# Mixer A's short tiles with both heads in one double bank, and late group norms finished one by one

## The chip, the cores and the metric

The kernel runs on one core of one Trainium2 chip. The metric is the device time of one execution in microseconds; the kernel before is given by the median of three runs. A profile is one further execution, taken by the hardware profiler, with its own time. TensorE (PE in the profile) does the matrix products, with its weight loads listed apart (PEld); VectorE (DVE), ScalarE (ACT) and GpSimd (POOL) do the elementwise work; SyncE (SP) issues the transfers.

## What is computed

One layer of a streaming encoder over 1024 prompt frames and 32 sample frames, with 1024 columns: a SwiGLU block, two attention mixers side by side, and a second SwiGLU block, each between a norm before it and a norm after it. What bears on the change is the middle part:

```python
qa, ka, va, qb, kb, vb = jnp.split(h @ w_in, SPLITS, axis=-1)
oa, ob, rows = mixers(qa, ka, va, qb, kb, vb)
o = jnp.concatenate([rmsnorm(oa, group_gains[:WIDTH_A]),
                     rmsnorm(ob, group_gains[WIDTH_A:])], axis=-1) @ w_out

def band_attn_a(q, k, v, bias, valid):          # mixer A: 8 heads x 64
    s = jnp.einsum('bnqhd,bnkhd->bnhqk', q, k) * SCALE + bias
    s = jnp.where(valid[None, :, None], s, NEG_INF)
    p = jax.nn.softmax(s, axis=-1)
    return jnp.einsum('bnhqk,bnkhd->bnqhd', p, v)
```

In mixer A a frame reads its own chunk of 64 frames and the eight chunks ahead of it, with a learned bias by distance. Mixer B is a narrower window with 8 query heads on 2 key heads. `o` is the concatenation of two normed groups of 512 columns: group 0 is mixer A's output, group 1 mixer B's.

## The kernel before

Columns stand on the partitions and frames along the free axis. Frames are cut into three blocks `tb`: 384, 384 and 288 (256 prompt frames and the 32 sample frames). Products of activations and weights are made with each operand split into a high and a low part, three products for one (`mm3`, lines 342 to 344: high by high, weight's high by the activation's low, weight's low by the activation's high). The weights are split on the chip as they arrive: ScalarE writes the high part (line 320), VectorE the low part (line 321).

**The attention part.** It goes through 72 tiles in a list written out by hand: mixer B's four pairs of heads, then mixer A's pairs 0 and 1, one after the other, then A's pairs 2 and 3 interleaved (numbers 54 to 71). A pair is one `TileS` (the sample frames) and eight tiles of 128 prompt frames, i = 0 to 7. A `TileA` with i = 0, 1, 2, 3 has L = 128, 256, 384, 512 keys; these are called the short tiles here. From i = 4 on L is 640. A tile has four steps:
- `pre` (POOL, lines 1104 and 1105): the queries of both heads into `qz`, zeros in the other head's rows.
- `qk(h)`, once for each head: the scores on PE into `S`, a PSUM double bank (line 1115), the bias added (DVE, 1117), the negated maximum (DVE, 1121), the exponential with its sum (ACT, 1124), the reciprocal (DVE, 1125), and the scaling of P (ACT 1127 or DVE 1129 in turn).
- `tr(h)`: P transposed on PE in blocks of 128 (`pp`, line 1139) and copied out (`evac`: ACT line 1068, every fifth DVE line 1066).
- `av`: P times V on PE (`po`, line 1076), and the copy of the result into `O`, again by `evac`.

`qk` of a tile comes one tile ahead of its `tr` and `av`; while pairs 0 and 1 run, the projections of later pairs (`pq`) are put between the tiles. PSUM is cut into three pools: `p2`, two double banks that hold scores; `p1`, three single banks; `pc`, one single bank.

**The output part.** `group_norm(tb, g)` norms a group of 512 columns of a block. ScalarE squares (line 381) two pairs of column tiles, `sumsq` adds the two of a pair (the fold, line 385) and the earlier pair to it (line 387), on POOL or DVE by the table `SQE`; PE sums over the partitions (`pss`, line 374); twelve small operations on DVE make the reciprocal root (lines 405 to 408 and 351 to 355, here the chain of the root); PE spreads it over the partitions (`pr`, line 422); ScalarE copies it to `rstd` (line 1523); DVE makes `z` (line 1528), ScalarE its high part `o_hi` (line 1532), and the low part `o_lo` (line 1533) is made on POOL for the first half and on DVE for the second. `out_piece` makes one 128-column piece of the product with `w_out` for one block (24 products `wo`), for which it needs both groups of the block.

**What sets the order.** The side jobs (norms, residuals) are generators in a list: `begin` puts one at its end, or with `first=True` at its front; `step` advances the frontmost; `need(key)` steps until one is done. The norms of group 1 are begun at tile 55. Group 0 of block 0 is begun at tile 63, of block 1 at tile 69, of block 2 after the last tile. Five output pieces go between the last tiles, the other nineteen after them. The tile library then assigns buffers, adds the waits, and orders the instructions of each engine by a simulated timeline of its own; each engine runs its own row of instructions in that order.

## Time and profile before

| what | value |
|---|---|
| runs | 2183.55, 2179.83, 2183.74 us, median 2183.55 |
| the profiled execution's own time | 2187.33 us |
| its span | 2185.4 us |
| its mean granted TensorE clock | 0.986 |
| PE, DVE, ACT, POOL busy | 2122.6, 1392.4, 778.5, 169.2 us |

A row of the groups reads: line, engine, operation, output and input with partitions by elements, count, busy time and mean of one, then the idle time of the engine ahead of them with what ended it. A row of the timeline reads: start, duration, engine, line, operation, count, and in brackets the wait ahead of it. A row of the windows gives the busy time of PE, PEld, DVE, ACT and POOL in a stretch with the count of instructions, then the granted clock, the share of the DMA engines and GB/s. The places of this text in that execution: pair 0 of mixer A opens at about 1065 us, pairs 2 and 3 at 1215 us, their first long tile is scored at 1254.8 us, the last `po` of the attention part runs at 1328 us, and the second SwiGLU block follows the norms from about 1350 us on.

### The profile page before, as it was taken

The numbers are of one execution on the slowest core, as the hardware profiler recorded it, in microseconds if no ns is written. First come the engines' busy times: TensorE is split into PE (matmuls) and PEld (weight loads), VectorE is DVE, ScalarE is ACT, GpSimd is POOL, SyncE is SP. The second block draws the span as 40 slices with busy tenths as digits, with TensorE's granted clock in tenths as the row PEclk, the third lists the DMA queues.
The fourth block names the chain that finished last, engine by engine and source line by source line (L and its number), as shares of the span: only waits on it lengthen the run. The fifth ranks groups of instructions, "written<-read, shape, count | busy, mean of one in ns | idle before, by whom it ended". The sixth has DMA issues, their size and how long they took to land.

```text
span 2185.4 us, 34225 instructions
## 1 busy us (share of the span) xinstructions
PE 2122.6 (97%) x13796; PEld 2029.9 (93%) x13796; DVE 1392.4 (64%) x2777; ACT 778.5 (36%) x1648; POOL 169.2 (8%) x273
## 2 busy tenths in 40 slices
PE   6999999999999999999999899999999999999998
PEld 4999999999999999988888579998999999999997
DVE  5687668756243387586644775689566656566657
ACT  3411111111121244476544674365432222233224
POOL 1100000000000022100100323320000000000001
PEclk9999999999999999999999899999999999999999
DMA  9343334423221244110210313254321111111114
GB/s 309 112 144 117 108 106 135 128 87 118 66 78 58 64 128 141 55 30 16 69 31 26 84 30 93 82 173 129 99 67 50 39 58 39 58 58 39 39 59 140
DMA packets 174355, 189.21 MB, mean 87 GB/s; under 512 B 7692, under 2 KB 143284, under 8 KB 173044
## 3 DMA queue, kind: packets, MB, share of 16 engines
q1 hardware_dynamic: 174196, 187.01, 27.5%
q8 instruction: 109, 1.79, 0.3%
q14 instruction: 50, 0.41, 0.1%
HBM read 167.27 MB, written 22.86 MB: 87 GB/s over the span
## 4 chain that ended last, share of the span: by engine, by line
PE 87%; DVE 6%; DMA 3%; ACT 2%; issue 1%; POOL 0%; SPq 0%; DVEq 0%; ACTq 0%; POOLq 0%
PE g L598 5%; PE up L344 4%; PE up L342 4%; PE up L343 4%; PE gate L344 4%; PE dn L342 4%; PE gate L343 4%; PE dn L343 4%; PE dn L344 4%; PE gate L342 4%; PE ga L598 3%; PE gd L598 3%; PE gb L598 3%; PE dn L810 3%; PE dn L808 3%; PE dn L809 3%
## 5 line engine op out<-in xcount | busy, mean ns | idle before, releaser
L321 DVE TENSOR_TENSOR w<-raw,w 128x1024 fp32r<-128x1024 f32 x102 | 125.1, 1231 | 75.2 <-ACT w L320 74.1
L808 PE MATMUL dn<-gg,w 128*128 128x384 f32 (+1 forms) x528 | 170.8, 324 | 1.3 <-DVE facc L815 1.3
L809 PE MATMUL dn<-gg,w 128*128 128x384 f32 (+1 forms) x528 | 169.7, 322 | 1.8 <-DVE gg L703 1.8
L810 PE MATMUL dn<-gg,w 128*128 128x384 f32 (+1 forms) x528 | 169.9, 323 | 1.2 <-DVE w L545 1.2
L544 ACT ACTIVATE w<-raw 128x512 fp32r<-128x512 f32 x180 | 110.1, 625 | 170.2 <-issue 75.8
L342 PE MATMUL dn<-gg,w 128*128 128x384 f32 (+1 forms) x528 | 169.7, 323 | 1.1 <-DVE facc L941 1.1
L343 PE MATMUL dn<-gg,w 128*128 128x384 f32 (+1 forms) x528 | 169.9, 322 | 0.0
L344 PE MATMUL dn<-gg,w 128*128 128x384 f32 (+1 forms) x528 | 169.4, 321 | 0.0
L385 POOL TENSOR_TENSOR sq<-sq 128x384 f32<-128x384 f32 (+1 forms) x48 | 51.8, 1088 | 1491.3 <-ACT sq L381 1467.4
L815 DVE TENSOR_TENSOR facc<-dn,facc 128x768 f32<-128x768 f32 (+1 forms) x120 | 106.6, 890 | 90.2 <-PE dn L810 90.2
L941 DVE TENSOR_TENSOR facc<-dn,facc 128x768 f32<-128x768 f32 (+1 forms) x120 | 106.1, 886 | 82.3 <-PE dn L344 82.2
L320 ACT ACTIVATE w<-raw 128x1024 fp32r<-128x1024 f32 x102 | 107.1, 1056 | 141.0 <-PE up L344 47.2
L245 DVE SCALAR_TENSOR_TENSOR macc<-raw,csil,macc 128x512 f32<-128x512 f32 x196 | 137.6, 745 | 15.1 <-DMA raw<-in_w_mod_dram 14.8
L545 DVE TENSOR_TENSOR w<-raw,w 128x512 fp32r<-128x512 f32 x180 | 124.7, 705 | 20.4 <-ACT w L544 20.1
L910 ACT ACTIVATE sl<-gate 128x384 f32<-128x384 f32 (+1 forms) x66 | 30.5, 462 | 281.3 <-PE gate L344 278.5
L598 PE MATMUL g<-h_hi,w 128*128 128x288 f32 x576 | 123.2, 294 | 0.0
L343 PE MATMUL gate<-h,w 128*128 128x384 f32 x352 | 118.4, 336 | 1.9 <-DVE h L470 1.9
L342 PE MATMUL gate<-h,w 128*128 128x384 f32 x352 | 118.7, 337 | 0.0
L344 PE MATMUL gate<-h,w 128*128 128x384 f32 x352 | 118.3, 336 | 0.0
L344 PE MATMUL up<-h,w 128*128 128x384 f32 x352 | 118.1, 336 | 0.0
L342 PE MATMUL up<-h,w 128*128 128x384 f32 x352 | 118.1, 336 | 0.0
L343 PE MATMUL up<-h,w 128*128 128x384 f32 x352 | 117.9, 335 | 0.0
(332 smaller groups left out, 5780.9 us busy)
## 6 DMA issues: line engine op xcount, KB each, us to landing
raw<-in_w_gate_dram SPq DMA_DIRECT2D x56, 512.0 KB, 3.9
raw<-in_w_up_dram SPq DMA_DIRECT2D x56, 512.0 KB, 4.0
raw<-in_w_down_dram SPq DMA_DIRECT2D x56, 512.0 KB, 3.7
raw<-in_w_mod_dram SPq DMA_DIRECT2D x56, 512.0 KB, 3.9
raw<-in_w_in_dram SPq DMA_DIRECT2D x18, 512.0 KB, 4.3
wm<-in_w_mod_dram SPq DMA_DIRECT2D x8, 1024.0 KB, 7.7
raw<-in_w_out_dram SPq DMA_DIRECT2D x13, 512.0 KB, 4.5
xr<-xs SPq DMA_DIRECT2D x16, 384.0 KB, 4.3
```

Of the source, the lines that this page charges most:

```text
L245: ve.scalar_tensor_tensor(acc[j], r[:, kk], c, acc[j], op0=OP.mult, op1=OP.add)
L320: ae.activation(w[:, 0], r, AF.Copy)
L321: ve.tensor_sub(w[:, 1], r, w[:, 0])
L342: te.matmul(ps, w[:, 0, k], hi, start=start, stop=False)
L343: te.matmul(ps, w[:, 0, k], lo, start=False, stop=False)
L344: te.matmul(ps, w[:, 1, k], hi, start=False, stop=stop)
L544: ae.activation(w[:, 0], src, AF.Copy)
L545: deferred.append(lambda: ve.tensor_tensor(w[:, 1], src, w[:, 0], op=OP.subtract))
L598: te.matmul(ps, w[a][:, k, :], x[b][k], start=first and k == 0 and q == 0, stop=last and k == n - 1 and q == 2, skip_group_check=True)
L808: te.matmul(ps[:, s, :w], h[:, k % 4, :], g[:, 0, :w], start=q == 0, stop=False)
L809: te.matmul(ps[:, s, :w], h[:, k % 4, :], g[:, 1, :w], start=False, stop=False)
L810: te.matmul(ps[:, s, :w], l[:, k % 4, :], g[:, 0, :w], start=False, stop=q == 1)
```

## The change

It has three parts.
- **Both heads in one double bank.** For a TileA with L up to 512, `qk(0)` now calls a new function `both`, and `qk(1)` does nothing. Both heads' scores go into the two banks of one `p2` buffer; the bias is added by one instruction over both heads, the maximum is made by one, the reciprocal by one. The exponentials and the scalings stay one for each head.
- **The late norms on VectorE.** `group_norm(1, 0)` and `group_norm(2, 0)` are called with `late`: their folds go to DVE instead of POOL, and so does the first half of `o_lo`; block 2's uses the bank of `pc` for `pss` and `pr` instead of one of `p1`.
- **One by one.** `need(("gn", 1, 0))` is called ahead of `begin(("gn", 2, 0), ...)`, so that block 1's norm is stepped to its end before block 2's is begun at the front of the list.

```diff
@@ -359,7 +359,7 @@
     def token_cols(w):
         return [(c, min(128, w - c)) for c in range(0, w, 128)]
 
-    def sumsq(src, kts, w, bank, ends, fold=True):
+    def sumsq(src, kts, w, bank, ends, fold=True, on=SQE):
 
 
         n = len(kts) // 2
@@ -380,7 +380,7 @@
             sq = h_tile([128, 2, 384], "sq")
             ae.activation(sq[:, :, :w], src[:, k:k + 2, :w], AF.Square)
             if fold:
-                e = SQE[c % len(SQE)]
+                e = on[c % len(on)]
                 e = ve if e == "v" else ge
                 e.tensor_tensor(sq[:, 0, :w], sq[:, 0, :w], sq[:, 1, :w], op=OP.add)
                 if acc is not None:
@@ -410,10 +410,10 @@
 
     waits = [0]
 
-    def mean_rstd(src, kts, w, scale, ends, bank=None):
+    def mean_rstd(src, kts, w, scale, ends, bank=None, on=SQE):
 
         bank = bank or pc
-        pss = yield from sumsq(src, kts, w, bank, ends)
+        pss = yield from sumsq(src, kts, w, bank, ends, on=on)
         y = rstd_cols(pss, w, scale)
         for _ in range(waits[0]):
             yield
@@ -1109,6 +1109,10 @@
             KQ = kqa[p][0]
             bias = prep[("A", p)]["bias"]
             bw = min(L, 256)
+            if L <= 512:
+                if h == 0:
+                    self.both(KQ, bias, bw)
+                return
             S = p2("S", (128, 1024))
             for c in range(0, L, 512):
                 ce = min(L, c + 512)
@@ -1128,6 +1132,27 @@
             else:
                 ve.tensor_scalar(P[:, :L], P[:, :L], den, None, op0=OP.mult)
             self.P[h] = P
+
+        def both(self, KQ, bias, bw):
+
+            i, k0, L = self.i, self.k0, self.L
+            S = p2("S2")
+            for h in range(2):
+                te.matmul(S[:, h, :L], self.T[:, h, :], KQ[:, 0, 128 * k0:128 * k0 + L], start=True, stop=True)
+            ve.tensor_tensor(S[:, :, L - bw:L], S[:, :, L - bw:L], bias[:, :, 256 - bw:256], op=OP.add)
+            nm = small.tile([128, 2], F32, name="nmb")
+            ve.tensor_reduce(nm, S[:, :, :L], axis=AX.X, op=OP.max, negate=True)
+            den = small.tile([128, 2], F32, name="denb")
+            self.P = [g_tile([128, 640], "P") for _ in range(2)]
+            for h in range(2):
+                ae.activation(self.P[h][:, :L], S[:, h, :L], AF.Exp, bias=nm[:, h:h + 1], accum_out=den[:, h:h + 1])
+            ve.reciprocal(den, den)
+            for h in range(2):
+                P = self.P[h][:, :L]
+                if (2 * i + h) % SC[1] < SC[0]:
+                    ae.activation(P, P, AF.Copy, scale=den[:, h:h + 1])
+                else:
+                    ve.tensor_scalar(P, P, den[:, h:h + 1], None, op0=OP.mult)
 
         def tr(self, h):
             P, nt = self.P[h], self.L // 128
@@ -1513,12 +1538,12 @@
 
     OH = [None] * 3
 
-    def group_norm(tb, g):
+    def group_norm(tb, g, late=False):
         w = TB[tb][1]
         if OH[tb] is None:
             OH[tb] = (u_tile(tb, "o_hi", F32R), u_tile(tb, "o_lo", F32R))
         hi, lo = OH[tb]
-        pr = yield from mean_rstd(O[tb], range(4 * g, 4 * g + 4), w, 2.0 / D, JG, p1)
+        pr = yield from mean_rstd(O[tb], range(4 * g, 4 * g + 4), w, 2.0 / D, JG, pc if late and tb == 2 else p1, 'v' if late else SQE)
         r = s_tile([128, 384], "rstd")
         ae.activation(r[:, :w], pr[:, :w], AF.Copy)
         for c in range(2):
@@ -1530,7 +1555,7 @@
             yield
             s = slice(4 * g + 2 * c, 4 * g + 2 * c + 2)
             ae.activation(hi[:, s, :], z[:, :, :w], AF.Copy)
-            (ge if c in GNP else ve).tensor_tensor(lo[:, s, :], z[:, :, :w], hi[:, s, :], op=OP.subtract)
+            (ge if c in GNP and not late else ve).tensor_tensor(lo[:, s, :], z[:, :, :w], hi[:, s, :], op=OP.subtract)
             yield
 
     wo, F2 = {}, [None] * 3
@@ -1627,7 +1652,7 @@
                     begin(("gn", tb, 1), group_norm(tb, 1))
             for tb in range(2):
                 if n == whole[tb] + 2:
-                    begin(("gn", tb, 0), group_norm(tb, 0), first=True)
+                    begin(("gn", tb, 0), group_norm(tb, 0, tb == 1), first=True)
             for _ in range(OUTS[n - 54] if n >= 54 else 0):
                 if outs and n >= whole[outs[0][0]] + 2:
                     out_piece()
@@ -1648,7 +1673,8 @@
                     fill(1e6)
                     budget = 0.0
     tiles[N - 1].av()
-    begin(("gn", 2, 0), group_norm(2, 0), first=True)
+    need(("gn", 1, 0))
+    begin(("gn", 2, 0), group_norm(2, 0, True), first=True)
     while outs:
         out_piece()
         step(OUTSTEP)
```

The number of instructions on PE (13,042 as the program lists them), ACT and SP stays as it was; DVE has 2739 for 2779, POOL 270 for 278. Lines behind the new function stand 25 higher in the kernel after: the transposes are on 1164 for 1139, `z`, `o_hi` and `o_lo` on 1553, 1557 and 1558, and the long tiles' scores on 1119; `both` has its scores on 1141, bias on 1142, maximum on 1144, exponential on 1148.

Three places show how the order of the instructions moves. The first is PE where pairs 2 and 3 open, behind the scores of the two sample tiles (`pps` are the sample tiles' transposes, `PTs` their P). Before:

```order
L1115 MATMUL S<-KQ,qz 128x128
L1076 MATMUL po<-PT,vt 64x128 x8
L1265 MATMUL pps<-ident,Ps 128x64 x4
L1266 MATMUL pps<-ident,Ps 32x64
L1076 MATMUL po<-PT,vt 64x128
L1115 MATMUL S<-KQ,qz 128x128
L1076 MATMUL po<-PTs,aux 64x32 x8
L1076 MATMUL po<-PTs,vs 64x32 x2
L1265 MATMUL pps<-ident,Ps 128x64 x4
L1266 MATMUL pps<-ident,Ps 32x64
L1115 MATMUL S<-KQ,qz 128x128 x2
```

The same place in the kernel after (the number behind S is the buffer's):

```order
L1141 MATMUL S_11830<-KQ,qz 128x128 x2
L1076 MATMUL po<-PT,vt 64x128 x7
L1290 MATMUL pps<-ident,Ps 128x64 x4
L1291 MATMUL pps<-ident,Ps 32x64
L1076 MATMUL po<-PT,vt 64x128 x2
L1141 MATMUL S_11880<-KQ,qz 128x128 x2
L1076 MATMUL po<-PTs,aux 64x32 x8
L1076 MATMUL po<-PTs,vs 64x32 x2
L1141 MATMUL S_11936<-KQ,qz 128x256 x2
```

Each buffer now takes both heads of a tile, and the first scores of L = 256 stand where the second sample tile's transposes stood.

The second place is PE behind the last `po`, where the norms of the late groups are summed and spread. Before:

```order
L344 MATMUL wo<-o_hi,w 128x384
L374 MATMUL pss<-ones,sq 128x1 x2
L374 MATMUL pss<-ones,sq 32x1
L422 MATMUL pr<-ident,ry 128x128 x2
L422 MATMUL pr<-ident,ry 128x32
L342 MATMUL wo<-o_hi,w 128x384
```

And after, where 47 `wo` products behind the last `po`, then a `pss`, 5 products, the other `pss` and 19 products stand ahead of these rows:

```order
L344 MATMUL wo<-o_hi,w 128x384
L422 MATMUL pr<-ident,ry 128x128 x2
L422 MATMUL pr<-ident,ry 128x32
L422 MATMUL pr<-ident,ry 128x128 x2
L422 MATMUL pr<-ident,ry 128x32
L342 MATMUL wo<-o_hi,w 128x384
```

Before, one group's `pr` stood directly behind its own `pss`, with 23 products between the last `po` and that `pss`; now both groups of block 2 are spread at one place, behind 19 products.

The third place is DVE at the same point of the program. Before:

```order
L321 TENSOR_TENSOR w<-raw,w 128x1024
L405 TENSOR_SCALAR rv<-pss 128x2
L406 TENSOR_SCALAR rv<-pss 32x1
L351 TENSOR_SCALAR ry<-rv 128x3
L353 TENSOR_TENSOR rt<-ry 128x3
L354 SCALAR_TENSOR_TENSOR rt<-rt,rv 128x3
```

After:

```order
L1553 SCALAR_TENSOR_TENSOR z<-o,cst,rstd 128x384 x4
L385 TENSOR_TENSOR sq<-sq 128x288
L321 TENSOR_TENSOR w<-raw,w 128x1024
L1558 TENSOR_TENSOR o_lo<-z,o_hi 128x768 x2
L385 TENSOR_TENSOR sq<-sq 128x288
L387 TENSOR_TENSOR sq<-sq 128x288
L405 TENSOR_SCALAR rv<-pss 128x2
L406 TENSOR_SCALAR rv<-pss 32x1
L405 TENSOR_SCALAR rv<-pss 128x2
L406 TENSOR_SCALAR rv<-pss 32x1
L351 TENSOR_SCALAR ry<-rv 128x3 x2
L353 TENSOR_TENSOR rt<-ry 128x3 x2
```

The folds of block 2 (128x288) and both halves of block 1's `o_lo` now stand in DVE's row, block 1's `z` ahead of them, and the two chains of the root for block 2 go step by step side by side.

## The prediction

> **What bounds the kernel now.** I read the page first: its busy line, then the chain of work that ended last.
>
> ```profile
> span 2185.4 us, 34225 instructions
> PE 2122.6 (97%) x13796; PEld 2029.9 (93%) x13796; DVE 1392.4 (64%) x2777; ACT 778.5 (36%) x1648; POOL 169.2 (8%) x273
> PE 87%; DVE 6%; DMA 3%; ACT 2%; issue 1%; POOL 0%; SPq 0%; DVEq 0%; ACTq 0%; POOLq 0%
> ```
>
> PE is 97% busy, and 87% of the chain lies on it. An instruction taken off another engine is worth nothing while PE has work, so the question is where PE starves and whether this change works there. The windows answer that (busy us of PE, PEld, DVE, ACT, POOL with counts, the granted clock, DMA share, GB/s):
>
> ```profile
> 1180.00:1200.00 20.00, 20.00 (x129) 16.13 (x128) 9.65 (x25) 8.42 (x19) 0.00 (x0) 1.00 0.23 67
> ...
> 1220.00:1240.00 20.00, 17.86 (x106) 11.76 (x102) 15.30 (x52) 12.65 (x38) 7.53 (x20) 0.66 0.35 103
> 1240.00:1260.00 20.00, 15.37 (x74) 8.51 (x75) 15.56 (x43) 12.26 (x30) 7.76 (x20) 0.83 0.00 0
> ...
> 1320.00:1340.00 20.00, 17.63 (x123) 16.13 (x122) 7.90 (x27) 7.88 (x15) 3.68 (x4) 0.92 0.34 105
> ```
>
> While pair 1 runs (first row) projections fill PE at the full clock: short tiles made cheaper there gain nothing. Where pairs 2 and 3 open (next two) no projection is left, and PE is idle in part and slow besides, at 0.66 and 0.83. In full-clock work PE did 17.86 x 0.66 + 15.37 x 0.83 = 24.5 us in 40: 15.5 us are lost. The last row is the end of the attention part, with a small loss. What PE waited for between 900 and 1500 us:
>
> ```profile
> PE po L1076 <- ACT o L1068: 4.5, 3, 3.1
> PE S L1115 <- ACT Ps L1251: 4.4, 2, 3.3
> PE pr L422 <- DVE ry L355: 2.4, 1, 2.4
> PE S L1115 <- POOL qz L1105: 1.2, 1, 1.2
> ...
> PE S L1115 <- ACT P L1124: 0.5, 1, 0.5
> ...
> PE pss L374 <- POOL sq L387: 0.3, 1, 0.3
> ```
>
> The change touches all of them: the `po` waits and the `qz` wait lie in the starved stretch, two openings have the sample tile's wait, a head's score waits once for an earlier exponential to free its buffer, and the last group norms have the wait for the root.
>
> **What both heads in one instruction save.** DVE's groups from 1040 to 1330 us:
>
> ```profile
> L1121 DVE TENSOR_REDUCE nm<-S 128x1 f32<-128x640 f32 x32 | 26.3, 820 | 0.6
> L1117 DVE TENSOR_TENSOR S<-S,aux 128x256 f32<-128x256 f32 x56 | 24.1, 431 | 42.0 <-PE S L1115 41.4
> ...
> L1125 DVE RECIPROCAL den<-den 128x1 f32<-128x1 f32 x64 | 10.0, 157 | 24.7 <-ACT P L1124 24.7
> L1121 DVE TENSOR_REDUCE nm<-S 128x1 f32<-128x512 f32 x8 | 5.5, 690 | 0.2
> L1121 DVE TENSOR_REDUCE nm<-S 128x1 f32<-128x384 f32 x8 | 4.4, 552 | 0.2
> L1180 DVE TENSOR_REDUCE nmb<-Sb 128x2 f32<-128x512 f32 x6 | 4.1, 687 | 0.1
> L1178 DVE TENSOR_TENSOR Sb<-Sb,bias 128x512 f32<-128x512 f32 x6 | 4.1, 690 | 1.1 <-PE Sb L1177 1.0
> ...
> L1121 DVE TENSOR_REDUCE nm<-S 128x1 f32<-128x256 f32 x8 | 3.4, 420 | 0.1
> L1117 DVE TENSOR_TENSOR S<-S,aux 128x128 f32<-128x128 f32 x8 | 2.4, 294 | 1.4 <-PE S L1115 1.3
> L1121 DVE TENSOR_REDUCE nm<-S 128x1 f32<-128x128 f32 x8 | 2.3, 282 | 0.1
> L1129 DVE TENSOR_SCALAR P<-P,den 128x512 f32<-128x512 f32 x4 | 2.2, 538 | 0.1
> ...
> L1190 DVE RECIPROCAL denb<-denb 128x2 f32<-128x2 f32 x7 | 1.1, 165 | 0.1
> ```
>
> Mixer B already uses the double form (1178, 1180, 1190), so its price stands here. A tile of 128 keys costs 2 x (294 + 282 + 157) = 1466 ns now, and 431 + 420 + 165 = 1016 after: 450 less. One of 256 costs 2 x (431 + 420 + 157) = 2016, then 690 + 687 + 165 = 1542: 474 less. For 384 and 512 the reduce runs over 768 and 1024, which no row shows; from 690 to 820 ns for 128 more I estimate 950 and 1210, hence 2 x (431 + 552 + 157) - (690 + 950 + 165) = 475 and 2 x (431 + 690 + 157) - (690 + 1210 + 165) = 491. Together 1.89 us a pair, 7.6 over four pairs, of which 3.8 in the starved stretch.
>
> In exchange the first exponential of a tile waits for both heads' bias and maximum. By the rows above that is, for 256 keys, 690 + 687 = 1377 ns behind the scores instead of 431 + 420 = 851: 0.5 us later, and some 0.6 later for 512. It is hidden where the tile behind it is already scored, and costs that much a tile, 4 to 5 us over the eight, where PE stands and waits for it. The buffers speak for the former: two double banks held one tile, a head in each, and now hold two tiles. The stretch on PE (start, duration, then the row):
>
> ```profile
> 1215.88 0.49 PE L1115 MATMUL S<-KQ,qz 128*128 128x128 f32 x2
> ...
> 1242.90 1.12 PE L1076 MATMUL po<-PT,vt 128*64 128x128 f32 x8 [3.06 <-ACT o L1068]
> ...
> 1254.79 1.32 PE L1115 MATMUL S<-KQ,qz 128*128 128x512 f32 x4 [1.21 <-POOL qz L1105]
> ```
>
> Eight short tiles take 38.9 us from the first score to the first long tile's. I split it at 1242.90. Ahead of it, ScalarE is held up by things that the change leaves:
>
> ```profile
> 1222.67 1.06 ACT L320 ACTIVATE w<-raw 128x1024 fp32r<-128x1024 f32 x1 [0.58 <-DMA raw<-in_w_out_dram]
> 1238.85 2.68 DVE L1528 SCALAR_TENSOR_TENSOR z<-o,cst,rstd 128x384 f32<-128x384 f32 x2
> ```
>
> The weight splits for `w_out` wait for their transfer, and the group norm's `z` occupies DVE, with ScalarE's `o_hi` behind it, up to the 3.06 us wait of `po`; after the change that eviction still stands behind two `o_hi`. I take 0 for these 27 us. Behind 1242.90 one head of 384 keys and four of 512 are scored in 11.9 us: the score of a head waits for the exponential of the head two before it. With a whole tile ahead, PE has a second tile's scores issued while DVE works on the first, and DVE's own work sets the pace: two tiles of 512 at 690 + 1210 + 165 = 2.07 us, half of one of 384 at 0.9, and three scalings of P at 0.54 are 6.7 us. With 0.2 between them I put the stretch at 6.9, **term A: -5 us**. Its bounds: +5, where the later exponential is waited for at every tile and the buffers give nothing; and, over the whole stretch, DVE's floor: 15.30 + 15.56 - 3.8 = 27.1 us of 40, that is -12.9. I take a value well inside since the stretch ahead of 1242.90 is bound by ACT and DVE together, and the one behind it by the buffers.
>
> **The late norms.** The tail on PE and DVE:
>
> ```profile
> 1332.83 0.76 PE L374 MATMUL pss<-ones,sq 128*128 128x1 f32 x6
> 1335.95 1.01 PE L422 MATMUL pr<-ident,ry 128*128 128x128 f32 x6 [2.37 <-DVE ry L355]
> 1336.89 0.69 PE L342 MATMUL wo<-o_hi,w 128*128 128x384 f32 x1
> ...
> 1340.26 0.34 PE L343 MATMUL wo<-o_lo,w 128*128 128x384 f32 x1
> ...
> 1341.83 0.33 PE L343 MATMUL wo<-o_lo,w 128*128 128x384 f32 x1
> ```
>
> ```profile
> 1333.62 0.16 DVE L405 TENSOR_SCALAR rv<-pss 128x2 f32<-128x2 f32 x1 [2.39 <-PE pss L374]
> ...
> 1335.64 0.16 DVE L355 SCALAR_TENSOR_TENSOR ry<-rt,ry 128x3 f32<-128x3 f32 x1
> ```
>
> PE has nothing between `pss` and `pr`: 2.37 us. Behind that its products are slow: ten from 1336.89 to 1340.26 take 3.37 us where nine from 1340.26 to 1341.83 take 1.57, so ten need 1.74 and 1.6 is lost. With the 0.3 of the `pss` that waits for POOL's fold, before loses 2.37 + 1.6 + 0.3 = 4.3 us. After the change, 19 products (19 x 0.174 = 3.3 us) stand between the second `pss` and the two `pr`, and two chains run side by side on DVE: the twelve steps of one took 1335.80 - 1333.62 = 2.18 us, so 22 to 24 steps take 4.0 to 4.4 if each costs the same, 2.2 if independent steps overlap. The new wait is 0 to 1.1; I take 0.9, near the upper end since the engine runs in order, and no slow clock behind it. **Term B: -3.4 us**, bounds -4.3 and 0.
>
> The Trainium skill ("TensorE: Matmul & The Clock Gate", Part 1, on oscillation) gives as the abstract rule that gaps above some 3.4 us throttle the clock. By it the 2.37 us would cost only itself, and term B would be some 1.5 smaller, -1.9. This trace's ten slow products behind 2.37 us speak against it.
>
> **What the late norms add on DVE.** Six folds and two halves of `o_lo` come over from POOL.
>
> ```profile
> 1362.60 0.55 DVE L385 TENSOR_TENSOR sq<-sq 128x384 f32<-128x384 f32 x1
> ...
> L1533 DVE TENSOR_TENSOR o_lo<-z,o_hi 128x768 fp32r<-128x768 f32 x3 | 3.7, 1221 | 0.0
> ```
>
> That is 6 x 0.55 + 2 x 1.22 = 5.7 us. DVE was busy 7.90 of 20 in the tail's window, so these lie beside PE's `wo` products: **term C: 0**. Without that cover they cost up to 5.7. A fold of block 1 stands between weight splits (321), and what is queued behind is the next split, for which `wo` products wait; in PE's row its `pss` stays where it was.
>
> **The rest.** Pair openings and the order of the heads of the second SwiGLU block shift by a few instructions. **Term D: 0**, within 1.5 both ways.
>
> The sum is -8.4 in the profiled execution's own time of 2187.33: 2178.9. That execution stands 3.78 above the median of the runs, 2183.55, so the forecast is **2175 us**.
>
> **The rivals.** All in the median's terms.
>
> *Only the tail gains* (term A at 0, the later exponential eating what the buffers give). For it: DVE is busy 15.56 of 20 there, so its order leaves little room. Against: PE is the one that stands behind DVE and ACT by turns, which is what a deeper buffer mends. 2183.55 - 3.4 = 2180.1.
>
> *Only the short tiles gain* (term B at 0). The double chain lies at 4.4 us and covers no less than the single one did, or a norm on DVE comes too late. Against: 19 products stand there. 2183.55 - 5 = 2178.5.
>
> *The whole stretch gains, down to DVE's floor*: -12.9 - 3.4, 2167.3. For it: eight tiles, all with a second buffer. Against: ScalarE's waits listed above.
>
> *Slower, from the openings of the pairs.* PE goes in order, and where pair 0 opens the scores of the sample tile and of three short tiles come ahead of projections:
>
> ```profile
> 1070.10 1.39 PE L1115 MATMUL S<-KQ,qz 128*128 128x128 f32 x4 [3.29 <-ACT Ps L1251]
> ```
>
> This wait for the sample tile's exponential was 3.29 us, 4.4 over two. Now the scores of 384 keys stand at the place of the second scores of the first tiles: they need both exponentials of the first tile, ahead of all projections. If a weight split that waits for its transfer comes ahead of these on ACT, the wait doubles: 4.4 more, and at each of the two openings 1.6 of slow clock as in the tail, +7.6. With the tail's -3.4 and nothing from term A, 2187.8; it decides from 3.4 us up. Against it: in ACT's row both exponentials stand ahead of the next split.
>
> *No net change*: 2183.5. DVE's work and the new order take as much as they give.
>
> **How the numbers follow.** Chances: forecast 0.40, only tail 0.17, only short tiles 0.10, down to the floor 0.12, slower 0.15, no change 0.06. 2166 to 2186 holds the forecast with its bounds, both one-sided cases, the floor, no change and the milder openings; what is left out is most of the slower case and a little on the lower side, together under 0.2. The difference that a measurement of this kernel can tell is about 0.2%, 4.4 us: faster is below 2179.2, slower above 2187.9. Faster: 0.34 of the forecast, 0.08 and 0.06 of the one-sided cases, 0.12 of the floor: 0.60. Slower: 0.12 of the openings' case. The rest, 0.28, is same.
>
> **What would show it.** Term A: from the `po` behind the `z` block to the first long score some 7 us instead of 11.9, and a higher granted clock from 1240 to 1260. The stretch ahead of it, 27 us, unchanged. Term B: the wait of `pr` for the root below 1.1 us and `wo` products at 0.17 behind it; no wait for POOL's fold. Term C: no wait of `wo` for `o_lo` or weights from DVE. Openings: the wait for the sample tile's exponential at or below 3.3 us. The prediction is wrong if the short stretch stays at 38.9, if the two chains cost PE over 2.4 us, or if a wait of over 3 us turns up in a place that had none.

## The result, and the profile after

The kernel after takes 2172.66 us (median of six runs, 2170.42 to 2175.45), the kernel before 2183.48 beside it (2179.83 to 2183.92): a ratio of 0.9951 with a 95% interval of 0.9941 to 0.9962, that is 10.8 us faster (8.3 to 12.9). The forecast was 2175 with a range of 2166 to 2186. A second measurement of both on another occasion gave 2173.28 against 2183.62, 0.9953 (0.9939 to 0.9967). So direction and size were right. How the terms were made up was right only in part.

The head of the page of the kernel after:

```profile
span 2173.7 us, 34152 instructions
PE 2117.1 (97%) x13796; PEld 2026.5 (93%) x13796; DVE 1388.0 (64%) x2737; ACT 775.5 (36%) x1648; POOL 158.2 (7%) x265
PE 85%; DVE 7%; DMA 4%; ACT 2%; issue 1%; POOL 0%; SPq 0%; DVEq 0%; ACTq 0%; POOLq 0%
```

VectorE has lost 4.4 us of work, GpSimd 11, and the span 11.7. To see where, I read the time of the same instruction in both traces at places where all work ahead of it is the same, and take the differences. Four stretches, in us (the kernel before was profiled a second time, see below; so was the change):

| stretch on PE | before | before, second | after | after, second |
|---|---|---|---|---|
| A's first sample scores to the first short score of pairs 2 and 3 | 151.19 | 150.82 | 150.38 | 150.64 |
| that short score to the last `po` | 111.52 | 111.57 | 109.59 | 108.98 |
| last `po` to the last `wo` product | 86.64 | 86.59 | 81.74 | 81.75 |
| last `wo` to the first product `ga` of the second SwiGLU block | 146.70 | 146.70 | 143.95 | 143.94 |

The tail gives 4.9 us, the starved stretch 2.3, the head of the second SwiGLU block 2.8, and the openings of pairs 0 and 1 some 0.5. That is 10.4 together. The two profiles of one kernel agree within 0.1 us in most of these stretches and 0.6 in the worst, while the whole spans of the two executions before differ by 5.0 us (2185.4 and 2180.4): 4.0 of these lie ahead of the first row of the table, where nothing is changed. Part of the 11.7 between the first two spans was thus that one execution.

**The tail.** In PE's timeline of the kernel after no wait is left at this place:

```profile
1333.53 0.65 PE L374 MATMUL pss<-ones,sq 128*128 128x1 f32 x6
...
1335.09 0.65 PE L374 MATMUL pss<-ones,sq 128*128 128x1 f32 x6
...
1339.09 1.91 PE L422 MATMUL pr<-ident,ry 128*128 128x128 f32 x12
1340.93 0.44 PE L342 MATMUL wo<-o_hi,w 128*128 128x384 f32 x1
1341.20 0.34 PE L343 MATMUL wo<-o_lo,w 128*128 128x384 f32 x1
```

```profile
1335.79 0.16 DVE L405 TENSOR_SCALAR rv<-pss 128x2 f32<-128x2 f32 x1 [1.35 <-PE pss L374]
...
1336.03 0.24 DVE L351 TENSOR_SCALAR ry<-rv 128x3 int32<-128x3 int32 x2
...
1337.80 0.23 DVE L355 SCALAR_TENSOR_TENSOR ry<-rt,ry 128x3 f32<-128x3 f32 x2
```

The second rows are DVE's: both chains of the root are done at 1338.03, 2.24 us behind the second `pss`, and a single chain took 2.18 before. Two steps that do not depend on each other (x2) take 0.23 us together. So the chains are over 1 us before PE comes to the `pr`, and the products behind it run at full speed.

**The starved stretch.** The windows of the kernel after, to be laid beside the ones shown of before (PE, PEld, DVE, ACT, POOL, granted clock, DMA share, GB/s):

```profile
1220.00:1240.00 20.00, 17.22 (x81) 11.28 (x81) 13.10 (x35) 12.79 (x40) 6.93 (x21) 0.58 0.28 84
1240.00:1260.00 20.00, 16.51 (x89) 10.40 (x86) 17.83 (x43) 12.86 (x32) 9.02 (x19) 0.91 0.00 1
...
1320.00:1340.00 20.00, 20.00 (x149) 18.76 (x147) 10.35 (x36) 9.14 (x17) 1.74 (x2) 1.00 0.34 106
```

The clock is not back in the first 20 us (0.58 for 0.66); in the next it is higher (0.91 for 0.83), and DVE is at 17.83 of 20. The prices of the double form were as worked out:

```profile
L1142 DVE TENSOR_TENSOR S<-S,aux 128x512 f32<-128x512 f32 x12 | 8.3, 694 | 12.0 <-PE S L1141 12.0
...
L1144 DVE TENSOR_REDUCE nmb<-S 128x2 f32<-128x1024 f32 x4 | 4.9, 1218 | 0.1
...
L1144 DVE TENSOR_REDUCE nmb<-S 128x2 f32<-128x768 f32 x4 | 3.8, 950 | 0.1
```

Estimated were 690, 1210 and 950. The first long score stands at 1248.81, 34.35 us behind the first short one where it was 38.9, so 4.6 us earlier by this mark (4.1 in the second profiles); but at the last `po` only 2.3 are left. The part from the `po` behind the `z` block, where the prediction split the stretch, to the first long score, before and after:

```profile
1242.90:1254.79 11.89, 10.15 (x39) 4.58 (x39) 8.50 (x22) 7.41 (x19) 5.73 (x15) 0.78 0.00 1
```

```profile
1242.36:1248.81 6.45, 4.45 (x32) 2.38 (x31) 6.42 (x11) 4.94 (x14) 4.99 (x15) 1.00 0.00 0
```

After the change VectorE is busy 6.42 of these 6.45 us. Not all of the difference is gained time: TensorE is busy 4.45 us here for 10.15, in part since some of its products now stand ahead of the first of the two marks. TensorE now runs ahead of it by a buffer, and part of that lead is paid back: behind the mark the second long score has a new wait. The profile names no releaser for it ("issue"), but the score starts 0.09 us behind the second exponential of the last short tile with the read of its sum, and I take it that it waits for that tile's buffer. ScalarE and PE:

```profile
1251.11 0.68 ACT L1148 ACTIVATE P<-S,nmb 128x512 f32<-128x512 f32 x1
1251.68 0.20 ACT L1148 ACTIVATION_READ_ACCUMULATOR P<-S,nmb 128x1 f32 x1
```

```profile
1251.97 1.32 PE L1119 MATMUL S<-KQ,qz 128*128 128x512 f32 x4 [1.49 <-issue]
```

From the first long score to the last `po` the change takes 75.2 and 74.1 us in its two profiles, where the kernel before takes 72.6 in both of its own.

A second new wait stands at the opening of the stretch. The scores of L = 256 are the third tile for two buffers. In the change's second profile (ScalarE, then PE):

```profile
1218.69 1.06 ACT L320 ACTIVATE w<-raw 128x1024 fp32r<-128x1024 f32 x1 [2.52 <-DMA raw<-in_w_out_dram]
1219.66 0.35 ACT L1148 ACTIVATE P<-S,nmb 128x128 f32<-128x128 f32 x1
...
1220.00 0.36 ACT L1148 ACTIVATE P<-S,nmb 128x128 f32<-128x128 f32 x1
1220.25 0.20 ACT L1148 ACTIVATION_READ_ACCUMULATOR P<-S,nmb 128x1 f32 x1
```

```profile
1220.55 2.05 PE L1141 MATMUL S<-KQ,qz 128*128 128x256 f32 x4 [3.24 <-issue]
```

The first tile's exponentials stand behind a weight split that waits for its transfer, and the scores start 0.1 us behind the second of them with the read of its sum. The wait is 3.24 us here and 2.26 in the first profile; the longest wait of the kernel before at this opening was 1.16 and 1.29 us in its two profiles. In exchange its wait of 3.06 us for `po` is gone.

**The head of the second SwiGLU block** was put at no change. There the kernel before has this wait, and the kernel after has a short one in its place:

```profile
1529.75 0.40 PE L598 MATMUL up<-h_hi,w 128*128 128x288 f32 x1 [1.53 <-ACT w L544]
```

```profile
1519.88 0.40 PE L598 MATMUL up<-h_hi,w 128*128 128x288 f32 x1 [0.25 <-ACT w L544]
```

Behind the 1.53 us PE's products stand 0.32 us apart for a time, behind the 0.25 us 0.17. The slow products are not what makes the difference, though: in the change's second profile they are there too, 3.4 us of them behind a wait of 1.82 us, the short waits behind them are gone, and the stretch is 143.94 all the same. On ScalarE two weight splits moved ahead of other work just ahead of the 1.53 us wait, and in PE's row, some 18 us behind it, four `dn` products moved ahead of a piece of the `gate` products. No line of the change stands in that part of the program.

### The profile page after: what moved, and what is told of

It reads as the page before. It is cut to its first block, busy times and chain, and to the rows that moved or that the text cites. A ratio compares the mean times of both kernels' runs of the same rounds, so it can differ in the third digit from the quotient of the medians.

```text
span 2173.7 us, 34152 instructions
## 1 busy us (share of the span) xinstructions
PE 2117.1 (97%) x13796; PEld 2026.5 (93%) x13796; DVE 1388.0 (64%) x2737; ACT 775.5 (36%) x1648; POOL 158.2 (7%) x265
## 3 DMA queue, kind: packets, MB, share of 16 engines
q1 hardware_dynamic: 174196, 187.01, 27.9%
## 4 chain that ended last, share of the span: by engine, by line
PE 85%; DVE 7%; DMA 4%; ACT 2%; issue 1%; POOL 0%; SPq 0%; DVEq 0%; ACTq 0%; POOLq 0%
PE g L598 5%; PE up L344 4%; PE up L342 4%; PE up L343 4%; PE ga L598 3%; PE gd L598 3%; PE gb L598 3%; PE dn L808 3%; PE gate L344 3%; PE dn L810 3%; PE gate L343 3%; PE dn L342 3%; PE dn L809 3%; PE dn L343 3%; PE gate L342 3%; PE dn L344 3%
## 5 line engine op out<-in xcount | busy, mean ns | idle before, releaser
L544 ACT ACTIVATE w<-raw 128x512 fp32r<-128x512 f32 x180 | 110.1, 626 | 170.6 <-issue 77.5
L815 DVE TENSOR_TENSOR facc<-dn,facc 128x768 f32<-128x768 f32 (+1 forms) x120 | 106.5, 890 | 89.7 <-PE dn L810 89.7
L320 ACT ACTIVATE w<-raw 128x1024 fp32r<-128x1024 f32 x102 | 107.1, 1056 | 142.2 <-PE up L344 47.2
L385 POOL TENSOR_TENSOR sq<-sq 128x384 f32<-128x384 f32 (+1 forms) x44 | 46.4, 1062 | 1506.8 <-ACT sq L381 1462.3
```

The lines of the kernel that those rows point to most:

```text
L320: ae.activation(w[:, 0], r, AF.Copy)
L544: ae.activation(w[:, 0], src, AF.Copy)
```

## The experiments

Each is given with its edit against the kernel after or before, and its time beside that of the kernel before, measured together with it. In what follows "the stretch" is the second row of the table above, "the tail" the third and "the head" the fourth.

**1. The double form alone.** Late norms as before:

```diff
-                    begin(("gn", tb, 0), group_norm(tb, 0, tb == 1), first=True)
+                    begin(("gn", tb, 0), group_norm(tb, 0), first=True)
...
-    need(("gn", 1, 0))
-    begin(("gn", 2, 0), group_norm(2, 0, True), first=True)
+    begin(("gn", 2, 0), group_norm(2, 0), first=True)
```

> The double form of the short tiles alone; the late norms as before. Reading A (the prediction's sizes): -5 us from the short tiles, tail unchanged with its 2.37 us wait, so 2178.5 against 2183.5. Reading B (the two traces): at equal work PE leads by some 2.4 us at the first output product (0.6 at the first opening, 1.3 to 1.6 in the starved stretch, the rest noise), nothing in the tail, so about 2181. Reading C (a rival): the buffers give nothing in the end, within 0.5 us of before. The wait of the first pr behind its pss stays at 2.4 us in all three; whether the head of the second SwiGLU block gains 2.5 us here as it did in the changed kernel is open, and if it does, that gain belongs to an earlier arrival and not to the norms.

2178.53 against 2183.13: 0.9977 (0.9967 to 0.9986), 4.6 us faster (3.1 to 7.2). The median fits reading A, but not for its reason: the stretch to the last `po` is 110.12 us, 1.4 shorter than before, the tail 87.36, 0.7 longer than before and with its wait, and the head of the second SwiGLU block 144.45, 2.25 shorter. That is reading B with the head's gain added. The head's open question is answered: the gain comes without the norms.

**2. The late norms alone.** Short tiles as before:

```diff
-            if L <= 512:
-                if h == 0:
-                    self.both(KQ, bias, bw)
-                return
```

> The late norms' part alone (VectorE, the other bank, one by one); the short tiles as before. Reading A: -3.4 us, 2180.1. Reading B: the tail gives what it lost, -4.7 us, and the head of the second SwiGLU block its 2.5, so -7.2, 2176.3. If the two parts add up, this run's difference and that of the double form alone make the whole change's -10.8.

2174.02 against 2183.13: 0.9956 (0.9941 to 0.9971), 9.1 us faster (6.3 to 12.9). Tail 81.75, head 143.93: reading B. The two parts do not add up: 4.6 + 9.1 is 13.7, the whole 10.8. The head's gain of 2.3 to 2.8 is in both and can be had once only: 13.7 - 2.4 = 11.3. Besides, the starved stretch took 108.38 us here with the old short tiles, row for row the program of before up to the last short tile, and 111.52 and 111.57 in the two profiles of before. TensorE's rows alone do not set it; see 8 and 9.

**3. The bank.** Block 2's late norm in the pool of three:

```diff
-        ..., JG, pc if late and tb == 2 else p1, 'v' if late else SQE)
+        ..., JG, p1, 'v' if late else SQE)
```

> The whole change, but block 2's late norm keeps its bank of the pool of three instead of the single one. By the prediction the distance between pss and pr came from the one-by-one order and from VectorE, so the tail would keep its gain: 2172.7. By the rival the bank is what lets products stand between pss and pr: with the old bank the row on PE has pr directly behind pss again, 24 products later than the last po, so the wait of 2.37 us and the ten slow products come back: about 4 us slower than the change, 2176.7.

2179.67 against 2183.13: 0.9986 (0.9976 to 0.9995), 3.5 us faster than before and about 7 slower than the change. The tail is 88.94 us, longer than before's 86.6. Its waits on PE:

```profile
PE pr L422 <- DVE ry L355: 2.4, 1, 2.4
PE pss L374 <- DVE sq L387: 2.1, 1, 2.1
```

In PE's row `pr` stands directly behind `pss` again, and the `pss` now waits for the folds that queue on VectorE too. The single bank is what lets products stand between the two.

**4. Without the one-by-one order** (short tiles as before):

```diff
-    need(("gn", 1, 0))
     begin(("gn", 2, 0), group_norm(2, 0, True), first=True)
```

> The late norms on VectorE with the single bank, but without finishing block 1's norm ahead of block 2's; short tiles as before. If the one-by-one order makes the gain: nothing in the tail, 2183. If the bank and VectorE make it: 31 and 24 products stand between pss and pr, no wait for the root, and -4 to -5 us as with all of the late part, 2179.

2189.64 against 2183.13: 1.0025 (1.0016 to 1.0035), 6.5 us slower than before and 15.6 slower than experiment 2, from which it differs by this line alone. Neither reading holds. The wait for the root is gone as the second says, but another takes its place. PE, ScalarE and GpSimd in its trace:

```profile
1347.25 1.21 PE L374 MATMUL pss<-ones,sq 128*128 128x1 f32 x6 [9.04 <-POOL sq L387]
```

```profile
1341.59 0.84 ACT L1553 ACTIVATE o_hi<-z 128x768 fp32r<-128x768 f32 x1 [0.38 <-DVE z L1549]
1342.64 0.84 ACT L1553 ACTIVATE o_hi<-z 128x768 fp32r<-128x768 f32 x1 [0.21 <-DVE z L1549]
1343.39 0.67 ACT L381 ACTIVATE sq<-o 128x576 f32<-128x576 f32 x1
```

```profile
1344.14 2.19 POOL L385 TENSOR_TENSOR sq<-sq 128x288 f32<-128x288 f32 x1 [42.71 <-ACT sq L381]
```

The second square of block 2's other group stands behind four `o_hi` on ScalarE (two are shown), its fold on GpSimd behind that, and PE waits 9.04 us for the sum. With block 1's norm finished first, the squares stand ahead of it. The tail is 93.9 us. So the bank and the order are needed together: each without the other loses the tail's gain.

**5. Without VectorE.** Folds and the first half of `o_lo` back on GpSimd, bank and order kept:

```diff
-        ..., pc if late and tb == 2 else p1, 'v' if late else SQE)
+        ..., pc if late and tb == 2 else p1, SQE)
...
-            (ge if c in GNP and not late else ve).tensor_tensor(lo[:, s, :], ...)
+            (ge if c in GNP else ve).tensor_tensor(lo[:, s, :], ...)
```

> The whole change, but the late norms' folds and the first half of the low part back on GpSimd; the single bank and the one-by-one order stay. On TensorE 18 products still stand between the second pss and the two pr. If the move to VectorE is needed for the tail's gain: the pss or the pr wait for GpSimd's fold, some 2 us, 2174.5 or more. If the bank and the order carry it alone: as the change, 2172.7.

2172.84 against 2183.62 (0.9953, 0.9941 to 0.9965), beside the change at 2173.28 measured together with it; the tail is 81.77 us. The move to VectorE is worth nothing, and cost nothing.

**6. The buffers without the double instructions.** Both heads of a short tile in one double bank, but bias, maximum and reciprocal one for each head:

```diff
+            for h in range(2):
+                ve.tensor_tensor(S[:, h, L - bw:L], S[:, h, L - bw:L], bias[:, h, 256 - bw:256], op=OP.add)
+                ve.tensor_reduce(nm[:, h:h + 1], S[:, h, :L], axis=AX.X, op=OP.max, negate=True)
...
+                ve.reciprocal(den[:, h:h + 1], den[:, h:h + 1])
```

> The whole change, with both heads of a short tile in one double bank, but bias, maximum and reciprocal again one for each head: the buffers alone, 0.47 us of VectorE a tile given back. If VectorE's price sets the pace of the starved stretch: up to 3.8 us slower than the change, 2176.5. If the buffers do it: as the change, 2172.7. If neither is worth anything there (the changed norms alone came to 2174.0): also 2172.7 to 2174.

2172.05 against 2183.30: 0.9952 (0.9937 to 0.9966), as the change. VectorE's 0.47 us a tile given back cost nothing that shows in the time. That they set no pace in the stretch does not follow: it took 107.05 us, less than the change's 109.0 to 109.6, but with the clock at half for 13.7 us instead of 17.1 and 20.5, and the part behind the `z` block's `po` took 6.9 us instead of 6.45. In PE's row at the head of the second SwiGLU block this kernel has the order of before, and there, alone of all that have the change's tail, it has no gain (146.35). So that gain goes with the order of a few instructions: every run with another order there has it (2.0 to 3.1 us), the kernel before and this one do not.

**7. The double form in pairs 2 and 3 only, and other scalings.**

```diff
-            if L <= 512:
+            if L <= 512 and p >= 2:
```

> The whole change, but the double form only in pairs 2 and 3; pairs 0 and 1, where projections fill TensorE, as before. The prediction says that the form is worth nothing in pairs 0 and 1 beyond their openings: within 1 us of the change, 2172.7. If the openings of pairs 0 and 1 carried what the double form alone gained (4.6 us), this run loses most of it and stands at 2175 to 2177.

2170.02 against 2183.30: 0.9936 (0.9924 to 0.9948). It loses nothing against the change; the form is worth nothing in pairs 0 and 1. Its stretch is 105.43 us, though all engines' rows of the first 40 us are the change's; the clock stood at half for 10.2 us of it instead of 20.5 and 17.1. The scalings half and half:

```diff
-                if (2 * i + h) % SC[1] < SC[0]:
+                if h == 0:
                     ae.activation(P, P, AF.Copy, scale=den[:, h:h + 1])
```

> The whole change, with the scaling of P in short tiles on ScalarE for the first head and on VectorE for the second, where two of three were on VectorE: 0.4 to 0.5 us of VectorE less in a third of the tiles' heads. VectorE was busy 17.8 of 20 us in the starved stretch after the change; if it is the bound there, 0.5 to 1 us faster, 2172; if ScalarE's queue is, as much slower, 2173.5.

2170.31 against 2183.30: 0.9936 (0.9924 to 0.9947), with a stretch of 106.52 us. That is 2.5 less than in the change's second profile, with the same 17.1 us at half clock; VectorE's saved time was to give 0.5 to 1, and what gives the rest stays open. Both edits in one kernel:

> The double form in pairs 2 and 3 alone, together with the scaling of P half and half: each alone came to 2170.0 and 2170.3. If the gains add: 2168. If each only moved the fall of the clock in the stretch to a better place: between 2167 and 2173, and the clock of the stretch tells which.

2170.28 against 2183.62: 0.9939 (0.9926 to 0.9952); the stretch is 105.01. The gains do not add.

**8. The kernel before again.**

> The kernel before, unchanged, profiled a second time: it tells how far one profiled execution stands for another. By the first reading of the traces the 3.06 us wait of po in the starved stretch and the 1.5 us wait with a slow clock at the head of the second SwiGLU block belong to the kernel, and both are here again. By the rival they belong to that one execution, since two kernels with the old short tiles had no such wait of po, and all four kernels run so far gain 2 us at that head whatever they change; then both are gone here and the milestones up to the last po lie 4 to 5 us earlier than in the first profile. Time 2183, same.

2182.41 against 2183.30, same (0.9996, 0.9987 to 1.0005). Both waits are here again:

```profile
1238.58 1.12 PE L1076 MATMUL po<-PT,vt 128*64 128x128 f32 x8 [3.07 <-ACT o L1068]
```

and at the head 1.55 us. At the head the first reading holds. The `po` wait goes with the old short tiles, but not in every execution: contrary to what was expected above, experiment 4 has it too (3.07 us), and of the four profiles with these rows on TensorE only experiment 2 does not. The milestones lie 4 us earlier, but this comes from ahead of all that the change touches.

**9. Work added.** By now the granted clock was the suspect. In windows of five us from the first short score, the clock of before reads 1.00, 0.50, 0.50, 0.64, 1.00, 0.54, 0.77 and then 1.00 (second profile); that of the change 1.00, 0.52, 0.50, 0.50, 0.77, 1.00, and from 35 us on 0.93 and 0.73 (first profile). In experiment 2, whose rows are before's, it reads 1.00, 0.61, 0.50, 0.50, 0.68, 1.00 without a second fall, and its wait of the `po` is 0.28 us instead of 3.07. So 27 products that nobody reads were put behind the scores of the first three short tiles of pairs 2 and 3:

```diff
                     self.both(KQ, bias, bw)
+                    if p >= 2 and i + p < 4:
+                        f = p1("fill")
+                        for j in range(9):
+                            te.matmul(f[:, :128], ident, ident, start=j == 0, stop=j == 8)
```

> The whole change with 27 products more, three times nine of the identity by itself into a bank that nobody reads, behind the scores of the first three short tiles of pairs 2 and 3: work added, nothing else changed. The rival that VectorE or ScalarE sets the pace of the stretch says: no gain, and up to 27 x 0.18 = 4.9 us lost. The theory that the granted clock sets it (TensorE at half speed and without a pause from 10 to 25 us behind the first short score, some 8 to 10 us lost) says: the idle time of 3 us that stands ahead of the fall is filled, the clock stays at or near 1.00, and the stretch gets shorter by more than the products cost, 1 to 5 us faster, 2168 to 2171.5.

The change itself, measured together with it:

> The change itself once more, as the measure for the three kernels beside it and as a second profile: 2172.7. In the starved stretch the granted clock by five-us windows from the first short score should again be about 1.00, 0.52, 0.50, 0.50, 0.8 and then near 1, with no second fall to 0.54 as in both profiles of the kernel before.

With the added work 2168.97, 0.9935 (0.9922 to 0.9947); the change 2173.28, 0.9953 (0.9939 to 0.9967). The intervals overlap a little; of the change's six times five lie above all six with the added products. The mean granted clock of these executions is 0.985 to 0.989 in the change and 0.989 to 0.994 with the products. The first three windows of ten us behind the first short score, of the change and of the kernel with the added products:

```profile
1212.56:1222.56 10.00, 6.06 (x61) 4.38 (x56) 6.40 (x12) 5.70 (x14) 3.69 (x4) 0.77 0.63 181
1222.56:1232.56 10.00, 8.89 (x44) 6.14 (x44) 7.03 (x23) 6.40 (x22) 5.73 (x15) 0.50 0.31 93
1232.56:1242.56 10.00, 9.62 (x53) 5.47 (x51) 8.37 (x16) 5.06 (x16) 4.88 (x14) 0.88 0.01 2
```

```profile
1213.74:1223.74 10.00, 10.00 (x117) 8.74 (x112) 7.36 (x14) 7.23 (x17) 2.22 (x4) 1.00 0.64 181
1223.74:1233.74 10.00, 8.67 (x64) 6.44 (x62) 8.34 (x27) 6.13 (x23) 6.88 (x19) 1.00 0.32 95
1233.74:1243.74 10.00, 9.31 (x55) 4.99 (x53) 10.00 (x17) 8.73 (x25) 7.02 (x15) 1.00 0.00 0
```

The 4 us in which PE was idle in the first ten are filled, and the clock does not fall at all. From the first short score to the last `wo` product it takes 187.0 us instead of 190.7. That is 3.7 us less with more work, while the clock alone had lost (1 - 0.77) + (1 - 0.50) + (1 - 0.88) of ten us each, 8.5. The rest went to the added products, which kept PE busy 6.7 us, some 4 of them in time that was idle before, and by the windows to VectorE, which is now busy 10.00 of 10 in the third: with the clock back, it is the next bound there. More differs than the products: the second sample tile's transposes stand ahead of the scores of L = 256 again, as in the kernel before (some rows of VectorE and ScalarE moved with them), and the wait of 2.3 to 3.2 us at these scores is gone. Experiment 6 has that order as well, and its clock stood at half for 13.7 us; so the order alone does not keep the clock up, but how much of the 3.7 us it gives is not shown.

All profiles of the stretch side by side, with the time at half clock from each trace's record of the granted clock:

| profiles | us at half clock in the stretch | the stretch, us |
|---|---|---|
| the kernel before, twice | 20.5, 20.5 | 111.5, 111.6 |
| experiments 2 and 4 (TensorE's rows as before) | 17.1, 17.1 | 108.4, 110.3 |
| the change, experiment 1 | 20.5, 20.5 | 109.6, 110.1 |
| the change again, experiments 3 and 5 (TensorE's rows as in the change) | 17.1, 17.1, 17.1 | 109.0, 108.7, 108.7 |
| experiment 6 | 13.7 | 107.1 |
| experiment 7: pairs 2 and 3, half and half, both | 10.2, 17.1, 13.7 | 105.4, 106.5, 105.0 |
| the added products | 0 | 105.3 |

Less time at half clock goes with a shorter stretch, but one order of instructions gives 108.4 to 111.6 us (first two rows, mean 110.4) and the other 108.7 to 110.1 (next two, mean 109.2). At equal clock, 20.5 us, the change's order is 1.4 to 2.0 us shorter; at 17.1 the two overlap.

## Why the prediction was right

*What bounds the kernel* was read rightly: PE fills pairs 0 and 1, and starves at the opening of pairs 2 and 3 and at the tail. Experiment 7 shows that the double form is worth nothing in pairs 0 and 1.

*Term A, -5 us for the short tiles.* Measured at the last `po`: -1.4 (experiment 1), -1.9 and -2.6 (the change's two profiles, against the two of before); by the means of all profiles with either order -1.2. The price on VectorE was right to 1%. At the marks that the prediction named the term even came true: from the `po` behind the `z` block to the first long score 6.45 us where 6.9 was forecast, with VectorE busy 6.42 of them, so its own work does set the pace there; and where experiment 7 takes scalings off VectorE this part falls to 5.4 and 4.8 us. The step that failed is the one from there to the kernel's time: what is gained up to the first long score was counted as gained for good. TensorE had run ahead of VectorE by a buffer; behind the mark its second long score waits 1.49 us, and up to the last `po` 2.6 and 1.5 us of the lead are lost again (in the first profile 1.7 of them by a second fall of the clock).

Ahead of the split, 27 us were to stay and 27.9 and 28.4 came out, but not for the reason given. The wait of 3.06 us for `po` was to stay and is gone; instead the scores of L = 256 wait 2.26 and 3.24 us, and the clock stands at half for 17.1 us there, for 15.3 before. The second profile's 3.24 us is a wait of over 3 us in a place that had no such wait, one of the signs by which the prediction was to be wrong. The granted clock was never priced in the term, although the windows quoted in the prediction show it at 0.66 and 0.83. Nor is a better clock shown to be what the buffers gave: the second fall is shorter in the change's first profile and in experiment 1 (3.4 us for 6.8), but the first fall is longer by as much (17.1 us for 13.7), and the sum is 20.5 as before. What is shorter at that equal clock, by an estimate from the traces that counts TensorE's busy time at half clock as half, is TensorE's own work in the stretch: 93.7 to 94.1 us in the five profiles with the change's rows, 95.1 to 95.5 in the four with the old ones, mostly in the scores and `po`. Why it is shorter stays open.

*Term B, -3.4 us for the tail.* Measured: -4.9. The mechanism was right: products between `pss` and `pr`, no slow clock behind. Two sizes were off. The new wait of 0.9 us is not there, since two chains side by side take 2.24 us, the lower end of the bounds; the choice "near the upper end since the engine runs in order" was wrong. And the loss before was some 0.6 more than the 4.3 summed up: the `wo` products take 1.9 us less after the change where 1.6 was put down for the slow clock, and the `pss` 0.3 less besides its wait. The sentence on the Trainium skill's throttle rule ("TensorE: Matmul & The Clock Gate", Part 1, on oscillation) stands as it was weighed: the slow products are in the second profile of before too, behind 2.36 us.

*Which edit carries the tail* the prediction did not separate. The single bank and the one-by-one order do, together; each alone makes the tail longer than before (experiments 3 and 4), and the folds on VectorE are worth nothing (5). *Term C, 0,* was right.

*Term D, 0 within 1.5,* was wrong: -2.8 at the head of the second SwiGLU block. The bound of 1.5 us had no row behind it, and the order of a few instructions elsewhere in the program was enough to move the waits of that place.

*The rivals.* Only the tail gains: nearest to what the last `po` shows of the short tiles, but with the head's gain unseen. Slower, from the openings: at pair 0 the wait for the sample tile's exponential is 2.7 and 3.0 us where it was 3.3, as ScalarE's row, both exponentials ahead of the next split, had said. At pairs 2 and 3 that rival's mechanism did come, a weight split waiting for its transfer ahead of the first tile's exponentials, and cost the 2.3 to 3.2 us at the scores of L = 256. That the sum came out right is luck in good part: term A was 2.7 us too large, terms B and D were 1.5 and 2.8 too small.

## What to carry to other kernels

Where an engine's granted clock is below 1 in a stretch, price the clock as well as the waits: what closes the gaps ahead of a fall counts there, and even useless products can pay. Read a gain at a mark where every engine has the same work behind it: a buffer more lets one engine run ahead, and what the other still has to do comes due behind the mark. For a wait on a chain of small dependent steps, look for what lets other work stand in the gap, a free bank and an order, before moving the steps to a faster engine. And profile both kernels twice before a difference of a few us at a place that the change does not touch is called a gain or a chance.

## What was unexpected of the hardware

How little idle time it takes for the clock to fall, and how long it stays down. The tail of the kernel before in windows of one us (PE, PEld, DVE, ACT, POOL, granted clock, DMA share, GB/s):

```profile
1335.00:1336.00 1.00, 0.05 (x1) 0.08 (x1) 0.66 (x5) 0.00 (x0) 0.00 (x0) 1.00 1.09 367
1336.00:1337.00 1.00, 1.00 (x7) 0.84 (x7) 0.00 (x0) 0.00 (x0) 0.00 (x0) 0.92 1.09 346
1337.00:1338.00 1.00, 1.00 (x3) 1.00 (x4) 0.56 (x2) 0.79 (x2) 0.00 (x0) 0.50 1.10 350
...
1340.00:1341.00 1.00, 1.00 (x7) 1.00 (x6) 1.00 (x1) 0.00 (x0) 1.00 (x1) 0.87 0.08 16
```

The fall comes 0.9 us after the wait has ended, while PE is already busy again, and lasts from about 1336.9 to 1340.3, some 3.4 us. In the starved stretch it comes 4.9 us behind the first short score in the kernel before, with no wait on PE ahead of it longer than 1.16 us, and lasts 13.7 us; in the change 17.1 us in both profiles, in experiment 2 also 17.1, with the double form in pairs 2 and 3 only 10.2. All are multiples of 3.41 us, while PE's rows show it busy for most of that time (11.7 of the 13.7 us). What counts as busy there the runs do not tell; with products of the identity in the gaps the clock did not fall.

Nor does the length of a wait alone decide. At the head of the second SwiGLU block one and the same wait of 1.82 us is followed by a fall of 3.4 us in the change's second profile and by none in its first. And row for row the same program on TensorE takes the stretch in 111.5, 110.3 or 108.4 us (the kernel before, experiments 4 and 2), with a second fall of the clock of 6.8 us, of 3.4 us, and none.

On VectorE, a step that needs the one before it starts 0.20 us behind it, two that don't 0.07 to 0.08 apart.
